# Orders of issue in the first stage of a hybrid retention and sparse-attention block: angle tables, variance, sine and gate stores

## The chip, the cores and the metric

The kernel runs on one core of a Trainium2 chip. The metric is device time in microseconds (us), the median of three runs. A core has five engines that run side by side and each issue their instructions in order: TensorE (PE, matmuls, and PEld, its weight loads), VectorE (DVE), ScalarE (ACT), GpSimd (POOL) and SyncE (SP), which here issues most transfers. They wait for each other through semaphores.

## The reference

One layer of a streaming encoder, 1024 positions of width 1024, all in float32. What matters here is its beginning:

```python
h = rms_norm(x, norm_mix)
proj = h @ w_in            # retention q, k, v, gate; sparse attention q, latent, k_pe, gate; indexer q, k, w
r_q, r_k = rotary(r_q, positions, 10000.0), rotary(r_k, positions, 10000.0)
q_pe, k_pe = rotary(d_q[..., :16], positions, 500000.0), rotary(d_pe, positions, 500000.0)
q_idx, k_idx = partial_rotary(i_q, ...), partial_rotary(i_k, ...)
ret = head_group_norm(retention(r_q, r_k, r_v), ret_norm) * silu(r_g)
score = sum over h of w_idx[h] * relu(q_idx[h] @ k_idx.T / sqrt(32))    # the indexer's scores
```

The 256 best keys of each query by `score` (chunk-causal) are attended to by the sparse heads; the outputs of both head groups go through an output projection, a gated embedding and a last norm. So the kernel needs the row's `rsqrt(mean(x*x))` (`rstd`), cosine and sine of two families of angles, the silu of the gate columns, and the indexer's rotated queries and keys before the first score.

## The kernel before

Matmuls of the projection run on split operands: each float32 is a high and a low part, and a product is three matmuls (high by high, high by low, low by high). The projection uses the unnormalised `x`; `rstd` is applied when a result is taken out of PSUM or through the angle tables.

The parts of the first stage, in the order of the program:

- Lines 288 to 300 load the transposed `x` in eight slices and the first weights `w_p1`, split them, and add up the squares in `acc`; `squares` is the last sum.
- Lines 305 to 314 accumulate the first projection block: two rotated halves in `P1` (PSUM tiles `big`) and the plain indexer columns in `PI[0]` (the two PSUM banks `nb`).
- `angles` and `tables` (lines 344 to 357) make a cosine and a sine table: VectorE multiplies the positions with the frequencies, reduces the angle to one turn in six instructions, ScalarE takes two sines and a square, VectorE makes the cosine of the square. `cosx`, `sinx` serve the sparse attention and the indexer, `cosr`, `sinr` retention.
- Lines 378 to 381 sum the squares over the partitions with matmuls (L380), and `rsqrt` makes `rstd`: a VectorE step (`rs_a`), a power on GpSimd (`rs_y`), four small VectorE steps. `spread` (line 364) spreads `rstd` over all partitions with matmuls (L368); ScalarE copies the result to `rstd_b`.
- `evacuate(0)` copies `PI[0]` to `it` on ScalarE (L375). It frees the two `nb` banks, which the gate chunk needs next.
- `t_block(12, ...)` is the second plain block of indexer columns; `put_plain` multiplies a block with `rstd_b`, splits it into `ih`, `il` and stores both to DRAM (`d_iq`, L407). `rotate` and lines 413 to 432 rotate `P1` (`xo`), split it (`xs`) and store the parts (`d_iq`, `d_ik`, `d_qs`, `d_kp`).
- `tables(cosr, sinr)` and their products with `rstd_b` (lines 433 to 435).
- Lines 446 to 474, the indexer's scores: `ks` and `qs` are loaded back from `d_ik` and `d_iq`, one matmul for each head (L466), a Relu on ScalarE (`rel`), a multiply-add on VectorE (`sc`).
- `n_chunk` (line 480): eight tiles of 128 rows and 256 columns, 24 matmuls each (L491 to L493), two tiles to a PSUM bank (`nb`, two buffers). ScalarE evacuates a tile with the chunk's function, for the gate chunks 2 and 3 the silu, into half of a buffer `nst` (three buffers, L495); GpSimd multiplies a full buffer with the norm's gain (L505), and SyncE stores it with two transfers (`d_g`, L510). Chunks run as 2, 3, 0, 1.

The program is not issued as written. A list scheduler puts the instructions of each engine in an order, by their place in the program and by when a model of their durations expects them to be ready; on the chip each engine then keeps that order, whatever is late. `with tc.issue_after(x)` and `add_manual_dep(..., NoSync, ...)` add an order of issue without a semaphore. `behind(ins, name)` notes an instruction, and `mark(name, last)` later orders all that were noted under that name behind `last`. The scores of the first two row tiles are so ordered behind the third tile of chunk 3 (`"chunk 3 tile 2"`).

Of the kernel before, what the change touches and what calls it, by code (L numbers as in the profile page):

```python
# [14 lines left out]
AF = mybir.ActivationFunctionType  # L15
# [138 lines left out]
def _body(ctx, nc, tc, ap, dbg):  # L154
    V, A, G, T, Y = nc.vector, nc.scalar, nc.gpsimd, nc.tensor, nc.sync

    def f(t):
        return t.bitcast(F32)
# [6 lines left out]

    def mark(name, ins):
        for x in marks.pop(name, []):
            tc.add_manual_dep(x.ins, ins.ins.name,
                              mybir.DependencyInfo(mybir.DependencyClass.NoSync, mybir.DependencyReason.DATA),
                              reason="order of issue")  # L170
# [157 lines left out]
    def rsqrt(out, ssum, n, w):  # L328
        a = tiny.tile([128, 16], F32, name="rs_a")[:, :w]
        y = tiny.tile([128, 16], F32, name="rs_y")[:, :w]  # L330
        z = tiny.tile([128, 16], F32, name="rs_z")[:, :w]
        V.tensor_scalar(a, ssum, 1.0 / n, EPS, op0=OP.mult, op1=OP.add)  # L332
        G.tensor_tensor(out=y, in0=a, in1=mhalf[:, :w], op=OP.pow)  # L333
        V.tensor_tensor(out=z, in0=y, in1=y, op=OP.mult)
        V.tensor_tensor(out=z, in0=z, in1=a, op=OP.mult)
        V.tensor_scalar(z, z, -0.5, 1.5, op0=OP.mult, op1=OP.add)
        V.tensor_tensor(out=out, in0=y, in1=z, op=OP.mult)
# [6 lines left out]
    def angles(col, cos_t):  # L344
        V.tensor_scalar(cos_t, posi, cst[:, CV + col:CV + col + 1], None, op0=OP.mult)

    def tables(cos_t, sin_t):
        ang, kk = cos_t, sin_t
        V.tensor_scalar(kk, ang, 1.0 / (2.0 * math.pi), MAGIC, op0=OP.mult, op1=OP.add)
        V.tensor_scalar(kk, kk, -MAGIC, None, op0=OP.add)  # L350
        for c in CODY:
            V.scalar_tensor_tensor(ang, kk, -c, ang, op0=OP.mult, op1=OP.add)
        V.tensor_scalar(ang, ang, PI_LO, -PI_LO, op0=OP.min, op1=OP.max)
        A.activation(sin_t, ang, AF.Sin)
        A.activation(cos_t, ang, AF.Sin, scale=0.5)
        A.activation(cos_t, cos_t, AF.Square)
        V.tensor_scalar(cos_t, cos_t, -2.0, 1.0, op0=OP.mult, op1=OP.add)

    with tc.issue_after(squares.ins):
        angles(1, cosx)  # L360
        tables(cosx, sinx)
        angles(0, cosr)

    def spread(dst, col):
        for h in range(2):
            pr = nb("ib")
            for j in range(4):
                T.matmul(pr[:, 128 * j:128 * j + 128], col[:, 4 * h + j:4 * h + j + 1].to_broadcast([128, 128]), ident,  # L368
                         start=True, stop=True)
            A.activation(dst[:, 512 * h:512 * h + 512], pr, AF.Copy)  # L370

    def evacuate(b):
        it = wk("it")
        for h in range(2):
            A.activation(it[:, 512 * h:512 * h + 512], PI[b][h], AF.Copy)  # L375
        return it
# [4 lines left out]
    rsqrt(rstd, pss[:, :NT], D, NT)  # L381
    spread(rstd_b, rstd)
    for t in (cosx, sinx):
        V.tensor_tensor(out=t, in0=t, in1=rstd_b, op=OP.mult)
    it0 = evacuate(0)
    PI.append([nb("ib"), nb("ib")])
    t_block(12, PI[1])
    it1 = evacuate(1)
# [13 lines left out]
    def put_plain(b, it):  # L402
# [3 lines left out]
        for n, t in enumerate((hi, lo)):  # L406
            Y.dma_start(d_iq[n, j0:j0 + nj].rearrange("j h t -> (j h) t"), f(t)[:8 * nj])  # L407
            if b == 1:
                Y.dma_start(d_ik[n, 8:32], f(t)[64:88])
# [23 lines left out]
    tables(cosr, sinr)  # L433
# [46 lines left out]
    def n_chunk(c, func, place=nb):  # L480
        ws = [load_w(ap["w_n"][c, kg], 256) for kg in range(4)]
        for tg in range(2):
            for a in range(4):
# [772 lines left out]
```

## Time and profile before

| | |
|---|---|
| median of three runs | 816.79 us (816.59 to 823.42) |
| the profiled execution | 815.47 us, of which 813.7 us from the first to the last instruction (the span) |
| TensorE busy | 755.0 us |
| VectorE busy | 587.5 us |
| ScalarE busy | 476.8 us |
| GpSimd busy | 312.5 us |
| mean granted TensorE clock | 0.977 of full |

All times inside the kernel are counted from the start of the span. The granted clock is the share of TensorE's full clock of 2.4 GHz that the chip allowed; 0.50 is its lower level, 1.2 GHz. A matmul's listed duration is longer than its distance from the next one, since matmuls are pipelined: distances between starts tell the pace. "Idle before" in a timeline is the time the engine stood still ahead of an instruction, with the instruction or transfer that ended it.

### The profile page before, as it was taken

The numbers are of one execution on the slowest core, as the hardware profiler recorded it, in microseconds if no ns is written. First come the engines' busy times: TensorE is split into PE (matmuls) and PEld (weight loads), VectorE is DVE, ScalarE is ACT, GpSimd is POOL, SyncE is SP. The second block draws the span as 40 slices with busy tenths as digits, with TensorE's granted clock in tenths as the row PEclk, the third lists the DMA queues.
The fourth block names the chain that finished last, engine by engine and source line by source line (L and its number), as shares of the span: only waits on it lengthen the run. The fifth ranks groups of instructions, "written<-read, shape, count | busy, mean of one in ns | idle before, by whom it ended". The sixth has DMA issues, their size and how long they took to land.

```text
span 813.7 us, 12654 instructions
## 1 busy us (share of the span) xinstructions
PE 755.0 (93%) x4415; PEld 653.5 (80%) x4415; DVE 587.5 (72%) x1270; ACT 476.8 (59%) x1041; POOL 312.5 (38%) x237
## 2 busy tenths in 40 slices
PE   9959499998999998999989888999999999899995
PEld 6858499987887887998788776878888887688885
DVE  5959058999999899999867877655565655644655
ACT  7544057638999599993666565543564544424333
POOL 2916245182765543740036668520261101310110
PEclk9969899998999999999999999999999999999999
DMA  8403733230532332531746565964445546542511
GB/s 317 123 21 109 189 101 96 78 98 27 145 114 79 117 104 89 173 119 52 194 111 189 171 190 162 268 233 149 160 168 191 168 163 218 195 156 78 180 52 52
DMA packets 65439, 113.89 MB, mean 140 GB/s; under 512 B 5888, under 2 KB 32896, under 8 KB 65376
## 3 DMA queue, kind: packets, MB, share of 16 engines
q1 hardware_dynamic: 61760, 106.53, 42.3%
q10 hardware_dynamic: 3616, 6.55, 2.2%
q8 instruction: 35, 0.57, 0.3%
q14 instruction: 28, 0.23, 0.1%
HBM read 75.45 MB, written 37.62 MB: 139 GB/s over the span
## 4 chain that ended last, share of the span: by engine, by line
PE 51%; DVE 31%; DMA 6%; ACT 4%; issue 4%; POOL 2%; SPq 1%; POOLq 0%; DVEq 0%; ACTq 0%
DVE res L645 8%; PE lg L1173 6%; PE rb L1173 5%; PE rb L1103 3%; PE rb L1104 3%; PE rb L1105 3%; DMA qk<-d_f 3%; PE tp L964 3%; DMA twr<-in_w_out 3%; PE nb L491 2%; PE nb L492 2%; PE nb L493 2%; DVE ad L654 2%; DVE sc L473 2%; DVE athr L656 2%
## 5 line engine op out<-in xcount | busy, mean ns | idle before, releaser
L235 POOL TENSOR_TENSOR wlo<-wraw,whi 128x512 fp32r<-128x512 f32 (+1 forms) x58 | 87.9, 1530 | 68.2 <-ACT whi L234 62.2
L661 ACT ACTIVATE ajunk<-key,cthr 128x1024 bf16<-128x1024 int16 (+5 forms) x96 | 95.5, 995 | 15.4 <-DVE key L622 10.5
L491 PE MATMUL nb<-whi,xhi 128*128 128x256 f32 x256 | 76.3, 300 | 22.8 <-ACT nst L495 14.1
L645 DVE TENSOR_SCALAR_CACHE_REDUCE res<-key,athr 128x384 f32<-128x384 int16 (+5 forms) x96 | 75.5, 786 | 2.1
L492 PE MATMUL nb<-wlo,xhi 128*128 128x256 f32 x256 | 75.6, 296 | 0.7 <-POOL wlo L235 0.7
L493 PE MATMUL nb<-whi,xlo 128*128 128x256 f32 x256 | 74.9, 295 | 0.0
L491 PEld LDWEIGHTS nb<-whi,xhi 128*128 128x128 f32 x256 | 52.1, 204 | 24.9 <-ACT nst L495 14.9
L333 POOL TENSOR_TENSOR rs_y<-rs_a,mhalf 128x1 f32<-128x1 f32 (+1 forms) x26 | 28.0, 1080 | 110.0 <-DVE rs_a L332 107.5
L971 DVE TENSOR_TENSOR t<-tp,t 128x512 fp32r<-128x512 f32 (+1 forms) x72 | 45.5, 643 | 29.7 <-ACT t L970 29.4
L947 ACT ACTIVATE lm<-lm,mxv 128x128 f32<-128x128 f32 (+3 forms) x64 | 49.4, 773 | 18.5 <-DVE mxv L946 17.0
L970 ACT ACTIVATE t<-tp 128x512 fp32r<-128x512 f32 (+1 forms) x72 | 38.9, 558 | 31.5 <-PE oo L1000 18.4
L322 PE MATMUL big<-xhi,whi 128*128 128x512 f32 x144 | 56.0, 391 | 0.5 <-DVE mb L399 0.5
L323 PE MATMUL big<-xlo,whi 128*128 128x512 f32 x144 | 56.2, 390 | 0.0
L324 PE MATMUL big<-xhi,wlo 128*128 128x512 f32 x144 | 55.7, 390 | 0.0
L473 DVE SCALAR_TENSOR_TENSOR sc<-rel,wi,sc 128x1024 f32<-128x1024 f32 (+5 forms) x42 | 51.0, 1214 | 4.3 <-ACT rel L469 1.6
L492 PEld LDWEIGHTS nb<-wlo,xhi 128*128 128x128 f32 x256 | 52.2, 204 | 1.9 <-POOL wlo L235 1.3
L493 PEld LDWEIGHTS nb<-whi,xlo 128*128 128x128 f32 x256 | 51.9, 203 | 0.6
L964 PE MATMUL tp<-cst,lm 128*128 128x128 f32 x288 | 46.8, 276 | 2.5 <-DVE t L971 2.0
L234 ACT ACTIVATE whi<-wraw 128x512 fp32r<-128x512 f32 (+1 forms) x58 | 34.9, 609 | 19.5 <-POOL cg L523 5.4
L943 DVE CUSTOM_DVE_ANT_0 lm<-lg,bias 128x512 f32<-128x512 f32 (+2 forms) x64 | 36.7, 585 | 11.9 <-PE tp L964 6.5
L1106 DVE TENSOR_TENSOR xt<-rb,xt 128x512 f32<-128x512 f32 x32 | 21.9, 689 | 30.3 <-PE rb L1105 25.9
L999 PE MATMUL oo<-t,vd 128*128 128x256 f32 (+1 forms) x144 | 38.1, 284 | 3.2 <-ACT t L970 2.9
(497 smaller groups left out, 2424.5 us busy)
## 6 DMA issues: line engine op xcount, KB each, us to landing
wraw<-in_w_t SPq DMA_DIRECT2D x26, 256.0 KB, 2.8
wraw<-in_w_n SPq DMA_DIRECT2D x24, 256.0 KB, 2.7
d_f<-o SPq DMA_DIRECT2D x8, 512.0 KB, 3.2
qk<-d_f SPq DMA_DIRECT2D x8, 512.0 KB, 4.9
ql<-d_qs SPq DMA_DIRECT2D x16, 256.0 KB, 4.5
qh<-d_qs SPq DMA_DIRECT2D x32, 128.0 KB, 4.9
twr<-in_w_out SPq DMA_DIRECT2D x8, 512.0 KB, 6.7
xt<-in_x SPq DMA_DIRECT2D x8, 512.0 KB, 4.3
```

What stands on the lines that cost most here:

```text
L235: G.tensor_tensor(out=lo, in0=raw, in1=f(hi), op=OP.subtract)
L322: T.matmul(outs[h], wh, xhi[k][:, sl], start=k == 0, stop=False)
L323: T.matmul(outs[h], wh, xlo[k][:, sl], start=False, stop=False)
L324: last = T.matmul(outs[h], wl, xhi[k][:, sl], start=False, stop=k == 7)
L473: V.scalar_tensor_tensor(dst, rel[:, :w], wi[:, i, h:h + 1], dst, op0=OP.mult, op1=OP.add)
L491: T.matmul(pb[:, a % 2], xhi[k][:, tsl], wh, start=k == 0, stop=False)
L492: T.matmul(pb[:, a % 2], xhi[k][:, tsl], wl, start=False, stop=False)
L493: last = T.matmul(pb[:, a % 2], xlo[k][:, tsl], wh, start=False, stop=k == 7)
L645: V.tensor_scalar(junk, src[:, KS[i]], thr[:, n:n + 1], 0.0, op0=op, op1=OP.add, accum_out=cnt[:, n:n + 1])
L661: A.activation(junk[:, :128 * (i + 1)], src[:, KS[i]], AF.Sign, bias=self.thr[:, n:n + 1], accum_out=cnt[:, n:n + 1])
L964: T.transpose(tp[:, o:o + 128], pt[a][:, ks_], ident)
L1173: T.matmul(po[c.start // 512][:, c.start % 512:c.start % 512 + c.stop - c.start], a, b[:, c], start=k == 0 and m == 0, stop=k == n - 1 and ...
```

## The change

Only orders of issue change; every instruction computes what it did.

1. In the first stage, after the sum of squares, VectorE is to do the first angle table (`cosx`) up to its last reduction (`reduced`), then the first step of `rsqrt` (`first`), then the angle of the second table (`turn`). The reductions of the second table come behind the last sum of the rotation (`turned`).
2. The first sine (`sine`) is issued behind the second copy of `it`.
3. The matmuls of the first `spread` are issued behind the last matmul of tile 0 of chunk 2.
4. The first store of the index path (the high part of `put_plain(0)`) is issued behind the second store of tiles 2 and 3 of chunk 2 (`"chunk 2 stored 3"`).

```diff
+    def queue(ins, first):
+        tc.add_manual_dep(ins.ins, first.ins.name, ...NoSync..., reason="order of issue")
...
-        V.tensor_scalar(a, ssum, 1.0 / n, EPS, op0=OP.mult, op1=OP.add)
+        first = V.tensor_scalar(a, ssum, 1.0 / n, EPS, op0=OP.mult, op1=OP.add)
...
+        return first, V.tensor_tensor(out=out, in0=y, in1=z, op=OP.mult)
...
-        V.tensor_scalar(ang, ang, PI_LO, -PI_LO, op0=OP.min, op1=OP.max)
-        A.activation(sin_t, ang, AF.Sin)
+        last = V.tensor_scalar(ang, ang, PI_LO, -PI_LO, op0=OP.min, op1=OP.max)
+        sin = A.activation(sin_t, ang, AF.Sin)
...
     with tc.issue_after(squares.ins):
         angles(1, cosx)
-        tables(cosx, sinx)
-        angles(0, cosr)
+        _, reduced, sine = tables(cosx, sinx)
+        turn = angles(0, cosr)
...
-    rsqrt(rstd, pss[:, :NT], D, NT)
-    spread(rstd_b, rstd)
+    first, scaled = rsqrt(rstd, pss[:, :NT], D, NT)
+    queue(first, reduced)
+    queue(turn, first)
+    spread(rstd_b, rstd, "chunk 2 tile 0")
...
-    it0 = evacuate(0)
+    it0, last = evacuate(0)
+    queue(sine, last)
...
-            Y.dma_start(d_iq[n, j0:j0 + nj].rearrange("j h t -> (j h) t"), f(t)[:8 * nj])
+            st = Y.dma_start(d_iq[n, j0:j0 + nj].rearrange("j h t -> (j h) t"), f(t)[:8 * nj])
+            if b == 0 and n == 0:
+                behind(st, "chunk 2 stored 3")
...
-        V.tensor_tensor(out=xo[:, :, sl], in0=two(ma), in1=two(mb), op=OP.add)
+        turned = V.tensor_tensor(out=xo[:, :, sl], in0=two(ma), in1=two(mb), op=OP.add)
...
-    tables(cosr, sinr)
+    first, *_ = tables(cosr, sinr)
+    queue(first, turned)
...
-                        Y.dma_start(dst[:, j - 1:j + 1], st.rearrange("p a (g c) -> g p a c", g=2)[a2])
+                        last = Y.dma_start(dst[:, j - 1:j + 1], st.rearrange("p a (g c) -> g p a c", g=2)[a2])
+                    mark(f"chunk {c} stored {j}", last)
```

## Rows read from the trace of the kernel before

**Rows 1.** The page: busy time and instructions by engine; granted clock in 40 slices.

```profile
PE 755.0 (93%) x4415; PEld 653.5 (80%) x4415; DVE 587.5 (72%) x1270; ACT 476.8 (59%) x1041; POOL 312.5 (38%) x237
...
PEclk9969899998999999999999999999999999999999
```

**Rows 2.** Timeline of TensorE: start us, us, instruction, idle before and its releaser.

```profile
50.29 0.58 PE L491 MATMUL nb<-whi,xhi 128*128 128x256 f32 x1 [8.73 <-ACT it L375]
...
56.32 0.28 PE L491 MATMUL nb<-whi,xhi 128*128 128x256 f32 x1
...
56.44 0.28 PE L492 MATMUL nb<-wlo,xhi 128*128 128x256 f32 x1
...
99.22 0.58 PE L491 MATMUL nb<-whi,xhi 128*128 128x256 f32 x1 [9.97 <-ACT nst L495]
...
108.59 1.09 PE L466 MATMUL big<-ks,qs 96*128 96x512 f32 x4
```

**Rows 3.** Stretches: us, busy us of PE, PEld, DVE, ACT, POOL (instructions); clock, DMA.

```profile
50.29:56.20 5.91, 5.91 (x27) 5.91 (x28) 1.57 (x6) 5.67 (x7) 2.06 (x2) 0.50 0.18 46
...
99.20:104.00 4.80, 4.78 (x22) 4.78 (x23) 0.00 (x0) 1.79 (x3) 2.39 (x2) 0.50 0.08 10
```

**Rows 4.** Timeline of ScalarE: the sine, a copy behind it, a table load.

```profile
48.70 1.06 ACT L354 ACTIVATE sinx<-cosx 128x1024 f32<-128x1024 f32 x1 [11.10 <-DVE cosx L353]
...
51.60 0.58 ACT L375 ACTIVATE it<-nb 128x512 f32<-128x512 f32 x1
...
60.12 1.28 ACT L495 ACT_TABLE_LOAD   x1
61.41 0.84 ACT L495 ACTIVATE nst<-nb,rstd 128x256 f32<-128x256 f32 x2
```

**Rows 5.** Timeline of VectorE: tables, variance, a product, the rotation's last sum.

```profile
34.26 1.78 DVE L345 TENSOR_SCALAR cosx<-posi,cst 128x1024 f32<-128x1024 int32 x1
...
39.36 0.68 DVE L349 TENSOR_SCALAR sinr<-cosr 128x1024 f32<-128x1024 f32 x1
...
42.30 1.21 DVE L352 SCALAR_TENSOR_TENSOR cosr<-sinr,cosr 128x1024 f32<-128x1024 f32 x1
...
49.18 0.15 DVE L332 TENSOR_SCALAR rs_a<-ib 128x8 f32<-128x8 f32 x1
...
51.71 0.17 DVE L337 TENSOR_TENSOR rstd<-rs_y,rs_z 128x8 f32<-128x8 f32 x1
...
63.54 1.22 DVE L435 TENSOR_TENSOR cosr<-cosr,rstd_b 128x1024 f32<-128x1024 f32 x1
...
74.81 3.42 DVE L416 TENSOR_TENSOR xo<-ma,mb 128x1024 f32<-128x1024 f32 x1
```

**Rows 6.** Timeline of SyncE's queue: index stores, weights, index loads, gate stores.

```profile
67.74 0.33 SPq L407 DMA_DIRECT2D d_iq<-ih  x1
...
71.48 2.69 SPq L231 DMA_DIRECT2D wraw<-in_w_n  x2
...
79.35 0.33 SPq L425 DMA_DIRECT2D d_iq<-xs  x1
...
91.75 0.56 SPq L453 DMA_DIRECT2D qs<-d_iq  x1
...
94.34 3.37 SPq L510 DMA_DIRECT2D d_g<-nst  x6
```

**Rows 7.** Chain of work, 30 to 125 us: start us, us, what.

```profile
94.99 3.60 DMA d_g<-nst
```

**Rows 8.** Waits, 30 to 125 us: total us, times, longest.

```profile
DVE sc L471 <- ACT rel L469: 27.4, 1, 27.4
```

**Rows 9.** Timeline of GpSimd: power of the variance, gate multiply of tiles 2, 3.

```profile
49.42 1.65 POOL L333 TENSOR_TENSOR rs_y<-rs_a,mhalf 128x8 f32<-128x8 f32 x1 [10.53 <-DVE rs_a L332]
...
81.71 2.27 POOL L505 TENSOR_TENSOR nst<-nst,retn_b 128x512 f32<-128x512 f32 x1
```

More of the change, by code (lines that the diff above doesn't have):

```diff
@@ L164, in behind @@
         marks.setdefault(mark, []).append(ins)
+    def queue(ins, first):
+        tc.add_manual_dep(ins.ins, first.ins.name,
+                          mybir.DependencyInfo(mybir.DependencyClass.NoSync, mybir.DependencyReason.DATA),
+                          reason="order of issue")
     def mark(name, ins):
         for x in marks.pop(name, []):
-            tc.add_manual_dep(x.ins, ins.ins.name,
-                              mybir.DependencyInfo(mybir.DependencyClass.NoSync, mybir.DependencyReason.DATA),
-                              reason="order of issue")
+            queue(x, ins)
     def pool(name, **kw):
@@ L336, in rsqrt @@
         V.tensor_scalar(z, z, -0.5, 1.5, op0=OP.mult, op1=OP.add)
-        V.tensor_tensor(out=out, in0=y, in1=z, op=OP.mult)
+        return first, V.tensor_tensor(out=out, in0=y, in1=z, op=OP.mult)
     cosr = rpool.tile([128, S], F32, name="cosr")
@@ L344, in angles @@
     def angles(col, cos_t):
-        V.tensor_scalar(cos_t, posi, cst[:, CV + col:CV + col + 1], None, op0=OP.mult)
+        return V.tensor_scalar(cos_t, posi, cst[:, CV + col:CV + col + 1], None, op0=OP.mult)
     def tables(cos_t, sin_t):
         ang, kk = cos_t, sin_t
-        V.tensor_scalar(kk, ang, 1.0 / (2.0 * math.pi), MAGIC, op0=OP.mult, op1=OP.add)
+        first = V.tensor_scalar(kk, ang, 1.0 / (2.0 * math.pi), MAGIC, op0=OP.mult, op1=OP.add)
         V.tensor_scalar(kk, kk, -MAGIC, None, op0=OP.add)
@@ L357, in tables, with spread @@
         V.tensor_scalar(cos_t, cos_t, -2.0, 1.0, op0=OP.mult, op1=OP.add)
+        return first, last, sin
     with tc.issue_after(squares.ins):
         angles(1, cosx)
-        tables(cosx, sinx)
-        angles(0, cosr)
-    def spread(dst, col):
+        _, reduced, sine = tables(cosx, sinx)
+        turn = angles(0, cosr)
+    def spread(dst, col, at=None):
         for h in range(2):
@@ L367, in spread @@
             for j in range(4):
-                T.matmul(pr[:, 128 * j:128 * j + 128], col[:, 4 * h + j:4 * h + j + 1].to_broadcast([128, 128]), ident,
-                         start=True, stop=True)
+                m = T.matmul(pr[:, 128 * j:128 * j + 128], col[:, 4 * h + j:4 * h + j + 1].to_broadcast([128, 128]),
+                             ident, start=True, stop=True)
+                if at:
+                    behind(m, at)
             A.activation(dst[:, 512 * h:512 * h + 512], pr, AF.Copy)
@@ L374, in evacuate @@
         for h in range(2):
-            A.activation(it[:, 512 * h:512 * h + 512], PI[b][h], AF.Copy)
-        return it
+            last = A.activation(it[:, 512 * h:512 * h + 512], PI[b][h], AF.Copy)
+        return it, last
     pss = nb("ib")
@@ L380, in _body @@
         T.matmul(pss[:, j:j + 1], acc[:, 128 * j:128 * j + 128], ones1, start=True, stop=True)
-    rsqrt(rstd, pss[:, :NT], D, NT)
-    spread(rstd_b, rstd)
+    first, scaled = rsqrt(rstd, pss[:, :NT], D, NT)
+    queue(first, reduced)
+    queue(turn, first)
+    spread(rstd_b, rstd, "chunk 2 tile 0")
     for t in (cosx, sinx):
         V.tensor_tensor(out=t, in0=t, in1=rstd_b, op=OP.mult)
-    it0 = evacuate(0)
+    it0, last = evacuate(0)
+    queue(sine, last)
     PI.append([nb("ib"), nb("ib")])
     t_block(12, PI[1])
-    it1 = evacuate(1)
+    it1, _ = evacuate(1)
     def two(t):
```

## The prediction, on record before the result was known

> **What bounds the kernel now.** I read the page first: TensorE is busy for 93% of the span and VectorE for 72%, so a gain has to come from TensorE's idle time or from work of VectorE that ends last. The page's clock line shows two places below full speed in the first eighth of the span [rows 1], so I went to the timeline of TensorE there. It has two holes. The first matmul of the gate stage (line 491) starts at 50.29 us after 8.73 us of idleness, and the view names ScalarE's copy `it` as what released it. A second hole of 9.97 us ends at 99.22 us, released by ScalarE's `nst` [rows 2]. Behind each hole the granted clock stands at 0.50 of full, that is 1.2 GHz: 27 matmuls take 5.91 us and 22 take 4.78 us [rows 3], where the same matmul later follows the one before it by 0.12 us (56.32 to 56.44) [rows 2]. At 0.12 us they would take 3.24 and 2.64 us, so the slow stretches cost 2.67 and 2.14 us.
>
> Why the first hole: ScalarE issues in order, and the sine of line 354 sits ahead of both copies of `it`. It waits 11.10 us for VectorE, runs at 48.70, and the copies follow, the second from 51.60 [rows 4]. VectorE is late because two angle tables go through it in turns: the first starts at 34.26 and the variance (`rs_a`) comes behind both at 49.18, so `rstd` is written only at 51.71 [rows 5].
>
> Why the second: `nst` has three buffers, and the evacuation of tile 6 needs the one whose two stores (`d_g`) stand in SyncE's queue behind all stores and loads of the index path. They are issued from 94.34 [rows 6], land 3.60 us after 94.99 [rows 7], and tile 7 of the same bank follows at 99.22 [rows 2]. VectorE meanwhile waits 27.4 us for the first scores [rows 8], which TensorE reaches at 108.59 [rows 2]. Both engines therefore wait for this stage, and what it loses shifts the rest of the kernel.
>
> **The change, part by part.**
>
> *One table first, variance between, sine behind the copies.* The copies of `it` need only the last projection matmuls. TensorE runs out of work at 50.29 - 8.73 = 41.56 us [rows 2]; the copies can be done by then, so the gate tiles start there instead of at 50.29, and at the full clock, since nothing has stood still. Gain: 8.73 + 2.67 = 11.4 us. `rstd` comes earlier too. From 34.26: one angle at 1.78, the two scalings at 0.68 to 1.78 each (0.68 is the row of the second table, 1.78 the first row, beside GpSimd's work), three of 1.21 and the clamp at 0.68 [rows 5], together 7.5 to 9.7; with the middle, 8.6, the table is reduced at 43 us. Then `rs_a` at 0.15, GpSimd's power at 1.65 [rows 9], and the steps up to `rstd`: in the trace `rs_a` to the end of `rstd` is 49.18 to 51.88, 2.7 us [rows 5]. `rstd` is there at about 46. The angle of the other table fits into the 1.65 of the power.
>
> *Spread behind tile 0.* 24 matmuls at 0.12 put the end of tile 0 at 41.56 + 2.9 = 44.5, and the spread that stands behind it waits for `rstd` until 46: a new wait of 1.5 us. If the compiled order puts tile 2 between, it is nothing; if `rstd` takes the long bound, 2.3. I take 1.5. Net of this part 9.9 us.
>
> *The second table behind the rotation.* Its six reductions move from before 49 us to behind the last sum `xo` (74.81) [rows 5]; one after another they are 5.7 us, and two products with `rstd_b` at 1.22 leave the stretch ahead of the rotation, which brings the index path forward by up to 2.4 us more. Cover: VectorE's 27.4 us of waiting for scores [rows 8]; the consumer, `cg` of retention (line 523), stands behind the score and value stages in the program. Without that cover the whole table costs 5.7 + 0.7 + 2.4 = 8.8 us of VectorE in a stage that it bounds. On ScalarE the split of the sines brings two more table loads, 1.28 us each [rows 4]. I take 0 for both, as the remaining hole (below) hides them, and up to 8.6 in a rival.
>
> *Gate stores ahead.* One store, the high half of the first index block (67.74 in the trace), is tied behind the second store of tile 3. The gate multiply that this store needs is at 81.71 for 2.27 us [rows 9], so done at 74.1 us once it is 9.9 us earlier. Three orders are possible in SyncE's queue. (a) The other index stores, being ready, go first; then gate stores of tiles 0 to 3, the tied store, and the loads `qs`. The gate stores then overtake only the four `qs` loads, 94.34 - 91.75 = 2.6 us [rows 6], and the hole shrinks from 9.97 to 7.4. (b) All of the index path waits for 74.1. The gate hole is then gone, but the queue's issues of 79.35 to 94.34, without a wait of some 2 us in them, are 13 us, and the earlier ones (two stores at 0.33, two weight loads in 2.69, a store pair of the like) some 4: `qs` would be issued at 91 and land some 4 us later (3.60 is the nearest row) [rows 6, 7], while TensorE, 22.0 us earlier than at 108.59, stands before its scores at 86.6: a hole of 8.4. (c) The gate stores slip in between the index stores at 70 to 75, nothing else waits, and next to nothing of the hole is left. I take (a), 7.4: a queue that has work of its own ready for 13 of 15 us leaves little room for (c).
>
> *Sum.* The holes and slow stretches are 8.73 + 2.67 + 9.97 + 2.14 = 23.5 us. Less 1.5 for the spread and 7.4 for the hole that stays: 14.6. The shorter hole need not bring the slow clock back; if it does, 2.1 of it are lost. All is read from one execution of 815.47 us (span 813.7, so 1.8 around it), 1.3 below the median of 816.79; the difference goes on the median: 816.8 - 14.6 = 802.2.
>
> **Rivals.**
>
> *Both holes close.* The gate stores leave at 70 to 75 and the index loads land before 87. For it: index data are ready earlier by 9.9 to 12.3 us, and the transfers themselves need 3.6. Against it: those 15 us of issues have one gap, of 2 us. 816.8 - 23.5 + 1.5 = 794.8.
>
> *Only the first hole closes.* The store order comes out as before, or the hole moves to the scores at full size with its slow clock. 816.8 - 9.9 = 806.9.
>
> *ScalarE waits for VectorE again.* The second pair of sines may be put ahead of an evacuation. It then waits for up to 5.7 us of the table, and its two loads (2.6) and three passes of 1.06 follow: 11.5 us, of which one tile (2.9) is covered by the other bank: 8.6 us, 810.8. Without the wait it is 2.9, and hidden in the hole. For it: the first hole is just this. Against it: nothing else of that stage is late, and an order made by a model can put the sines where the table is done. The Trainium skill speaks against the change here: "ScalarE: Activation LUTs", section "Table sets: the hidden batching unit", says to batch by table set, and this splits one batch of sines into two. The same page, section "What ACT_TABLE_LOAD costs", adds 1.38 us of drain to each load; by that it would be 813.6. Here the first evacuation starts 1.29 us after its load starts (60.12 to 61.41) [rows 4], so the row shows the load alone.
>
> *Slower: the whole index path is held by the gate store.* If (b) holds and the gate multiply itself comes late on GpSimd, every microsecond passes on to the scores. In (b) the scores come about 21 us after the store; they are no earlier than the present 108.59 when it leaves at 88 us, and the kernel is 1% slower (825) from 96 us on. For it: one queue, in order. Against it: the multiply is at 81.71 even now, and its inputs come earlier.
>
> **How the numbers follow.** Chances: forecast 0.47 (798 to 806), both holes closed 0.22, only the first 0.11, ScalarE again 0.12, slower 0.08. The likeliest is 802.2. The range runs from nothing new lost, 816.8 - 23.5 = 793, to the ScalarE case with a little more, 812; what is left out is the slower case and some of the ends, under 2 in 10. A change of 1% (8.2 us) is about what a measurement of this kernel can tell from none: faster means below 808.6. That holds for the forecast, for both holes closed and for part of "only the first": 0.74. Same 0.18, slower 0.08.
>
> **What would show it.** TensorE's first gate matmul at 41.6 instead of 50.29 with no slow stretch behind it; `rs_a` near 43 and `rstd` near 46; a sine that starts behind both copies of `it`; the second table on VectorE between the last `xo` and the first score; `d_g` stores in SyncE's queue ahead of `qs`; a hole of some 7 us, before tile 7 or before the first scores, which come near 94. I am wrong if the first gate matmul still waits, if the scores do not come at least 10 us earlier, or if the later stages, which the change does not touch, give the shift back.

## The result, and the profile after

| | before | after |
|---|---|---|
| median of four runs on one chip | 819.44 us (816.59 to 823.42) | 808.08 us (806.26 to 811.39) |
| the profiled execution | 815.47 us, span 813.7 | 808.18 us, span 806.4 |
| mean granted clock | 0.977 | 0.980 |

The ratio of the times is 0.9871, with a 95% interval from 0.9835 to 0.9906: the change takes off 1.3%, 11.4 us between the medians. The forecast was 802.2 with a range of 793 to 812. Some executions below ran in a slower state of the chip and are left out of every median and ratio; of the first and the fourth experiment only times are told, since the profiled execution was one of these.

The page of the changed kernel, its busy times and its clock line (to be held against [rows 1]):

```profile
PE 755.7 (94%) x4415; PEld 656.1 (81%) x4415; DVE 591.8 (73%) x1270; ACT 477.0 (59%) x1041; POOL 313.2 (39%) x237
...
PEclk9999799999999999999999999999999999999998
```

No engine does less; TensorE stands still less. The low slice of the clock line that came from the first hole is gone, and the one in the fifth slice has stayed. The timeline of TensorE, changed kernel (start us, us, instruction, idle before and its releaser), answers [rows 2]:

```profile
41.28 0.36 PE L504 MATMUL nb<-whi,xhi 128*128 128x256 f32 x1
...
48.92 2.02 PE L373 MATMUL ib<-cst,rstd 128*128 128x128 f32 x16 [1.64 <-issue]
...
52.97 0.40 PE L326 MATMUL ib<-xhi,whi 128*128 128x512 f32 x1
...
84.30 0.58 PE L504 MATMUL nb<-whi,xhi 128*128 128x256 f32 x1 [5.08 <-ACT nst L508]
...
96.73 1.17 PE L479 MATMUL big<-ks,qs 96*128 96x512 f32 x4 [3.29 <-DMA qs<-d_iq]
```

Stretches of the same kernel (us, busy us of PE, PEld, DVE, ACT, POOL with instructions; granted clock; DMA share; GB/s), against [rows 3]:

```profile
41.28:47.28 6.00, 5.99 (x50) 5.79 (x49) 4.36 (x7) 3.18 (x4) 2.47 (x2) 1.00 0.18 44
84.30:88.20 3.90, 3.90 (x18) 3.90 (x19) 1.45 (x2) 2.98 (x4) 1.33 (x2) 0.51 0.88 224
...
98.40:101.80 3.40, 3.40 (x18) 3.40 (x17) 2.98 (x3) 1.99 (x4) 0.00 (x0) 0.50 0.36 127
```

The first gate matmul starts 9.0 us earlier, at 41.28, with no wait over 0.6 us ahead of it, and at full clock. Two waits are left in series where the second hole was: 5.08 us on a gate evacuation and 3.29 us on the query load. Behind each the clock is at half, behind the first at once, behind the second from 98.40, 1.7 us after the wait ended. At 0.12 us a matmul, 18 would take 2.16 us; they take 3.90 and 3.40, so the slow stretches cost 1.74 and 1.24.

These rows close the sum of the first stage. Before, the two holes and their slow stretches were 23.5 us. After, the waits ahead of the first score are 1.64 + 5.08 + 3.29 = 10.01 and the slow stretch between them 1.74, together 11.75. The difference is 11.8, and the first score comes 108.59 - 96.73 = 11.9 us earlier. With the 1.24 behind the scores, 10.5 us remain: VectorE's twenty-first multiply-add of the scores follows at 134.49 instead of 144.80, 10.3 earlier. The end of this execution is only 7.3 us earlier than that of the execution before, so in this pair the later stages give back 3.0 us; among other things the granted clock is 0.97 from 430 to 490 us and 0.93 from 490 to 515, where it was 1.00 in these stages before, and TensorE waits 3.5 us on `vd` at line 761, where the longest such wait was 1.6 before. But the execution before lay 4 us below its median, with a mean clock of 0.977, as high as any execution of that kernel shows. Between the medians (11.4 us, by the interval 7.7 to 13.5) a loss behind the first stage does not show; one trace of each does not settle whether a typical execution has one.

ScalarE, changed kernel, against [rows 4]:

```profile
40.13 0.58 ACT L382 ACTIVATE it<-nb 128x512 f32<-128x512 f32 x1
...
44.77 1.06 ACT L358 ACTIVATE sinx<-cosx 128x1024 f32<-128x1024 f32 x1 [2.75 <-DVE cosx L357]
...
48.89 1.28 ACT L508 ACT_TABLE_LOAD   x1 [0.88 <-DVE rstd L341]
...
76.99 0.47 ACT L508 ACTIVATE nst<-nb,rstd 128x256 f32<-128x256 f32 x1 [5.45 <-PE nb L506]
82.82 1.06 ACT L358 ACTIVATE sinr<-cosr 128x1024 f32<-128x1024 f32 x1 [5.36 <-DVE cosr L357]
83.79 0.46 ACT L508 ACTIVATE nst<-nb,rstd 128x256 f32<-128x256 f32 x1
```

The first sine stands behind both copies, as meant. The second sine stands ahead of an evacuation (83.79) and waits 5.36 us for VectorE: this is the wait of 5.08 on TensorE. Between the evacuation at 76.99 and this sine there is no table load.

VectorE, changed kernel, against [rows 5], then GpSimd, against [rows 9]:

```profile
44.65 0.16 DVE L336 TENSOR_SCALAR rs_a<-ib 128x8 f32<-128x8 f32 x1
...
48.05 0.69 DVE L361 TENSOR_SCALAR cosx<-cosx 128x1024 f32<-128x1024 f32 x1 [0.47 <-ACT cosx L360]
48.65 0.16 DVE L341 TENSOR_TENSOR rstd<-rs_y,rs_z 128x8 f32<-128x8 f32 x1
...
67.27 2.32 DVE L428 TENSOR_TENSOR xo<-ma,mb 128x1024 f32<-128x1024 f32 x1
69.51 2.89 DVE L353 TENSOR_SCALAR sinr<-cosr 128x1024 f32<-128x1024 f32 x1
...
72.44 1.67 DVE L354 TENSOR_SCALAR sinr<-sinr 128x1024 f32<-128x1024 f32 x1
74.03 3.42 DVE L430 TENSOR_TENSOR xs<-xo,xs 128x1024 fp32r<-128x1024 f32 x1
```

```profile
44.89 2.09 POOL L337 TENSOR_TENSOR rs_y<-rs_a,mhalf 128x8 f32<-128x8 f32 x1 [3.22 <-DVE rs_a L336]
...
71.81 1.74 POOL L518 TENSOR_TENSOR nst<-nst,retn_b 128x512 f32<-128x512 f32 x1
```

`rstd` is 3.1 us earlier than before, and its last step stands behind the cosine of the first table (48.05), which waits for ScalarE's square. Two reductions of the second table (69.51 and 72.44) stand between the last sum `xo` and its split `xs`, which is what the index path waits for. SyncE's queue and the chain of work, changed kernel, against [rows 6, 7]:

```profile
68.53 1.58 SPq L523 DMA_DIRECT2D d_g<-nst  x2
...
86.27 0.94 SPq L523 DMA_DIRECT2D d_g<-nst  x2
87.25 0.50 SPq L417 DMA_DIRECT2D d_iq<-ih  x1
...
90.76 0.56 SPq L466 DMA_DIRECT2D qs<-d_iq  x1
```

```profile
69.59 2.82 DVE sinr L353
...
87.25 3.50 DMA d_iq<-ih
91.36 5.23 DMA qs<-d_iq
```

The gate stores of tiles 0 and 1 leave at 68.53, ahead of nearly the whole index path; those of tiles 2 and 3 leave at 86.27, then the tied store, and the query load can go only when that store has landed (87.25 + 3.50 = 90.75). The chain that ended last runs through just these: the reductions, the tied store, the query load. And the cover of [rows 8] has shrunk from 27.4 us to 7.8 (the wait of VectorE's first score step in the list of waits; the store named there is what came last by the profile, not what the step needs):

```profile
DVE sc L484 <- DMA d_g<-nst: 7.8, 1, 7.8
```

### The profile page after: what moved, and what is told of

Same layout as the page of the kernel before. It is cut to its first block, busy times and chain, and to the rows that moved or that the text cites. A ratio compares the mean times of both kernels' runs of the same rounds, so it can differ in the third digit from the quotient of the medians.

```text
span 806.4 us, 12657 instructions
## 1 busy us (share of the span) xinstructions
PE 755.7 (94%) x4415; PEld 656.1 (81%) x4415; DVE 591.8 (73%) x1270; ACT 477.0 (59%) x1041; POOL 313.2 (39%) x237
## 4 chain that ended last, share of the span: by engine, by line
PE 62%; DVE 18%; DMA 8%; ACT 4%; issue 3%; POOL 2%; SPq 1%; ACTq 0%; POOLq 0%; DVEq 0%
PE lg L1187 6%; PE rb L1187 5%; PE rb L1117 4%; PE rb L1118 4%; PE rb L1119 4%; PE tp L978 3%; PE big L328 3%; PE big L327 3%; PE big L326 3%; DVE res L659 3%; PE nb L504 2%; PE nb L505 2%; PE nb L506 2%; DMA qk<-d_f 2%; DMA twr<-in_w_out 2%
## 5 line engine op out<-in xcount | busy, mean ns | idle before, releaser
L675 ACT ACTIVATE ajunk<-key,cthr 128x1024 bf16<-128x1024 int16 (+5 forms) x96 | 95.5, 995 | 14.9 <-DVE key L636 10.5
L504 PEld LDWEIGHTS nb<-whi,xhi 128*128 128x128 f32 x256 | 50.9, 199 | 10.8 <-ACT nst L508 9.7
L486 DVE SCALAR_TENSOR_TENSOR sc<-rel,wi,sc 128x1024 f32<-128x1024 f32 (+5 forms) x42 | 51.0, 1214 | 5.8 <-ACT rel L482 3.0
L957 DVE CUSTOM_DVE_ANT_0 lm<-lg,bias 128x512 f32<-128x512 f32 (+2 forms) x64 | 36.7, 584 | 13.5 <-PE tp L978 7.5
L978 PEld LDWEIGHTS tp<-cst,lm 128*128 128x128 f32 x288 | 34.7, 144 | 8.7 <-DVE t L985 5.3
```

The costliest lines, as they stand in the source:

```text
L486: V.scalar_tensor_tensor(dst, rel[:, :w], wi[:, i, h:h + 1], dst, op0=OP.mult, op1=OP.add)
L504: T.matmul(pb[:, a % 2], xhi[k][:, tsl], wh, start=k == 0, stop=False)
L675: A.activation(junk[:, :128 * (i + 1)], src[:, KS[i]], AF.Sign, bias=self.thr[:, n:n + 1], accum_out=cnt[:, n:n + 1])
L978: T.transpose(tp[:, o:o + 128], pt[a][:, ks_], ident)
```

## The experiments

The theory after the result: the first hole was closed by the orders on VectorE and ScalarE; of the second hole, one part is now the second sine waiting for its reductions, the other the query load waiting for the tied store. The rival: what is left of the second hole is still the gate stores' place in SyncE's queue. The experiments undo or add one part at a time. "First score" is the first matmul of line 479 in the changed kernel.

One fact of the compiled programs matters throughout. An edit in the first stage can change the order that the list scheduler gives to the stages long behind it. For each kernel I compared the order of TensorE's instructions with that of the changed kernel, by tenths of the program (1.00: all stand in the same order):

```
kernel before                 .80 .99 1.0 1.0 1.0 1.0 1.0 1.0 1.0 1.0
without the tie               same as changed in all tenths
sine behind tile 6            same as changed in all tenths
sine behind tile 7 (1 and 3)  1.0 .45 .59 .99 .99 1.0 .54 .60 .85 .85
first sine free (7)           .92 1.0 1.0 1.0 1.0 1.0 .54 .60 .85 .85
sine alone (8), and run 4     .99 1.0 1.0 1.0 1.0 1.0 .65 .54 .85 .85
tie alone (9)                 .80 1.0 1.0 1.0 1.0 1.0 .60 .51 .85 .85
```

Runs 1, 3 and 7 have the very same order in the last four tenths; runs 4 and 8 share another, run 9 has a third. The order in which the matmuls start in the traces groups the kernels in the same way. Kernels without a line here (6, 10, 11, 12) keep the changed kernel's order behind the first two tenths.

**Run 1: the second sine later.** To take the wait of 5.36 off the evacuations:

```diff
-    first, *_ = tables(cosr, sinr)
+    first, _, sine = tables(cosr, sinr)
+    behind(sine, "chunk 2 taken 7")    # marked at the evacuation of tile 7
```

> The changed kernel with one edit: the second pair of sines is ordered behind the evacuation of tile 7 of chunk 2, so that ScalarE no longer waits 5.36 us for VectorE ahead of the evacuation of tile 6. Theory (two waits in series on the way to one event, the first scores, and the later one, the loads qs that land near 96.6 us, decides): the hole of 5.08 us before 84.30 goes, TensorE reaches the scores near 87 and waits there until 96 to 97, the first score stays at 96.7 within 1 us and the time within 2 us of the changed kernel (806 to 810). Rival (ScalarE's wait is what keeps the gain from its forecast size): the first score comes at 90 and the time falls by 5 to 7 us, to 801 to 803.

818.79 us, ratio to before 1.0025 (0.9995 to 1.0055): the whole gain is gone. Neither theory foresaw that. It led to the comparison of the compiled orders, and to runs 5 and 7.

**Run 2: without the tie of the first index store.**

```diff
-            if b == 0 and n == 0:
-                behind(st, "chunk 2 stored 3")
```

> The changed kernel without the tie of the first index store to the gate stores of tiles 2 and 3 (the other orders stay). Theory (the gate stores of the first two tiles come early because their evacuation does, not because of the tie; the tie only puts 3.5 us of a late store ahead of the loads qs): qs are issued near 86.5 instead of 90.8, the first scores come 2 to 4 us earlier (93 to 95), the gate stores of tiles 2 and 3 land near 92 and hold the evacuation of chunk 3's first tile by 2 to 4 us; the time is 804 to 808. Rival (the tie is what shrinks the second hole): a hole of 7 us or more returns before tile 7 and the time is 811 or more.

803.63 us, ratio 0.9828 (0.9789 to 0.9867). SyncE's queue and TensorE of this kernel:

```profile
85.74 0.56 SPq L464 DMA_DIRECT2D qs<-d_iq  x1
```

```profile
83.76 0.58 PE L502 MATMUL nb<-whi,xhi 128*128 128x256 f32 x1 [5.08 <-ACT nst L506]
```

The query load leaves 5.0 us earlier than with the tie, and the wait of 3.29 ahead of the scores is gone; the first score is at 93.57. The gate stores of tiles 0 and 1 still leave at 68.01. So the tie costs 3.2 us at the first score, and the early gate stores don't come from it. The differences of the medians are 2.2 apart, the same way, but less than their uncertainty. The later stores now hold an evacuation of ScalarE for 3.11 us, as expected, but TensorE does not wait for it. The wait of 5.08 is unchanged, which excludes the rival: the gate stores are early, and the evacuation waits all the same.

**Run 3: run 1, and the second table's reductions behind the split.** `queue(first, turned)` becomes `queue(first, parted)`, where `parted` is the last instruction that writes the low half of `xs`.

> As the late sine, and the reductions of the second table are ordered behind the split of the rotated block (xs) on VectorE instead of behind its sum xo. Theory (two of these reductions, 2.82 and 1.61 us, stand between xo and its split and hold the whole index path): the split starts near 70.7 instead of 74.03, every store behind it and the loads qs come 3 to 4 us earlier, the first score near 93, and the time is 803 to 806. Rival (SyncE's queue and the transfers set when qs land, not the split): the first score stays at 96 to 97 and the time at 806 to 810.

The first stage did as the theory said: the split at 70.38 instead of 74.03, the first score at 93.00, 15.6 us earlier than before. The time did not: 817.85 us, ratio 0.9997 (0.9973 to 1.0021). The loss lies hundreds of microseconds later. TensorE's two longest waits there, in this kernel:

```profile
477.43 0.61 PE L850 MATMUL rb<-cst,qk 128*128 128x128 f32 x3 [4.08 <-DMA qk<-d_f]
...
537.01 0.79 PE L1119 MATMUL rb<-wo0h,mTh 128*128 128x512 f32 x1 [5.29 <-ACT mTh L1109]
```

Neither the kernel before nor the changed one has a wait over 2.5 us on TensorE between 400 and 610 us.

**Run 4: run 3 with the tie moved to the stores of tiles 0 and 1** (`"chunk 2 stored 1"`).

> As the last, and the first index store is tied behind the stores of tiles 0 and 1 only. Theory (the late tied store, 3.5 us to land, stands ahead of qs): qs are issued near 83 and land near 88, TensorE reaches the scores at 87, the first score comes at 88 to 90 and the time is 798 to 802. Rival (the gate stores of tiles 2 and 3, now behind qs, hold the evacuations of chunk 3): a hole of 5 us or more opens around the first scores, and the time is 803 to 808.

802.98 us, ratio 0.9822 (0.9783 to 0.986), between the two ranges expected. It differs from run 3 in one order, the gate stores behind which the first index store stands, and is 14.9 us faster. In the first stage run 3 has only one wait over 1.6 us left (2.35 us, ended at 88.63, with a granted clock of 0.68 in the 5.4 us behind it), so the first stage can account for some 4 us at most. That the rest is the other order of the later stages was inferred here; runs 5 and 7 test it.

**Run 5: the second sine behind tile 6.** Run 1 with `"chunk 2 taken 6"`; the later order is that of the changed kernel.

> The changed kernel with the second sine ordered behind the evacuation of tile 6 of chunk 2 instead of tile 7 (that was the earlier run with the late sine); here every engine's compiled order behind the first stage is the one of the changed kernel. Theory (the late sine lost its gain because the scheduler re-ordered the later stages): the wait of 5.08 us before the tile at 84.30 shrinks to 0 to 3, the query load still leaves near 90 because it stands behind the tied store, so the first score comes at 94 to 97 and the time is 804 to 808. Rival (a late second sine costs time by itself, for instance because its table is late for whoever reads it): 815 to 820, as the run with tile 7.

807.88 us, ratio 0.986 (0.9797 to 0.9924), against 818.79 for run 1, which places the same sine one tile later. A late sine does not cost the gain by itself: here it kept it, and in run 3, with the sine behind tile 7, the first score came 15.6 us earlier. What runs 1 and 3 have and this run has not is the other later order. TensorE of this kernel:

```profile
85.35 0.58 PE L505 MATMUL nb<-whi,xhi 128*128 128x256 f32 x1 [3.46 <-ACT whi L238]
...
95.85 1.16 PE L480 MATMUL big<-ks,qs 96*128 96x512 f32 x4 [2.92 <-DMA qs<-d_iq]
```

As for the first stage, the wait of 5.08 became one of 3.46 on converted weights, which stand behind the sine on ScalarE, and the scores still wait for the query load (2.92): the first score is at 95.85, only 0.9 us earlier than in the changed kernel, since the load, behind the tied store, sets it.

**Run 6: no tie, and the reductions behind the split.**

> The changed kernel without the tie of the first index store, and with the second table's reductions behind the split of xo instead of behind xo; every engine's compiled order behind the first stage is the one of the changed kernel. Theory (reductions of 4.6 us in front of the split delay the index path by some 3.5): the split at 70.4 instead of 73.5, the query load at 82 to 83 instead of 85.7 of the run without the tie; the first score at 89 to 92 (93.57 there), 799 to 802. Rival (the transposing engine's own wait for the second sine sets the scores, and that waits for the same reductions, now later): first score at 93 to 95, 803 to 806.

800.16 us, ratio 0.9784 (0.9732 to 0.9836): the lowest time of the study, 18.5 us below the medians of before. VectorE and TensorE of this kernel:

```profile
70.42 2.22 DVE L428 TENSOR_TENSOR xs<-xo,xs 128x1024 fp32r<-128x1024 f32 x1 [1.03 <-ACT xs L427]
```

```profile
84.30 0.51 PE L503 MATMUL nb<-whi,xhi 128*128 128x256 f32 x1 [2.51 <-ACT whi L238]
...
86.17 0.58 PE L504 MATMUL nb<-wlo,xhi 128*128 128x256 f32 x1 [1.36 <-POOL wlo L239]
```

The split is 3.1 us earlier than in run 2 and the query load leaves at 83.30, 2.4 us earlier. The first score, at 92.69, gains only 0.9, since TensorE is now late by itself: behind the second sine, which still waits for VectorE, stand the weight conversions of the next chunk. That is the rival's mechanism and the theory's time; the first score lies between the two ranges. The median is 3.5 us below that of run 2, more than the first score shows; each has an uncertainty of some 4 us.

**Run 7: the changed kernel without the order of the first sine** (`queue(sine, last)` left out).

> The changed kernel without the edit that queues the first sine behind the copies. The compiled order still has both copies ahead of the sine, so the first stage keeps its gain (first gate matmul at 40 to 42, first score at 94 to 99); but behind tenth 6 of the program the compiled order of every engine is the one of the two slow runs with the late sine, not that of the changed kernel. Theory (that order costs 11 to 14 us between 430 and 600): 815 to 821. Rival (the order of the later stages costs nothing, and those runs lost for another reason): 806 to 811.

Ratio 1.0028 (0.9995 to 1.0061), median 821.89. Two things are read from it, and one of them goes against the text of the expectation, which was wrong on the compiled order: without the edit the sine stands ahead of the copies. TensorE of this kernel:

```profile
46.83 0.58 PE L503 MATMUL nb<-whi,xhi 128*128 128x256 f32 x1 [5.58 <-ACT it L382]
...
483.44 0.90 PE L847 MATMUL rb<-cst,qk 128*128 128x128 f32 x3 [5.30 <-DMA qk<-d_f]
...
542.53 0.50 PE L1116 MATMUL rb<-wo0h,mTh 128*128 128x512 f32 x1 [3.77 <-ACT mTh L1106]
```

First, one angle table first, without the order of the sine, shortens the first hole from 8.73 to 5.58 and no more. Second, the scores come 7.3 us earlier than before and the kernel ends later than before: the two long waits of run 3 are here too, on the same lines of the program, with the same later order and another first stage. Held against the shift of the first scores (the table below), this later order costs 10 us here and 16 in run 3; which difference in it makes the load of `qk` late was not followed.

**Run 8: the order of the first sine alone**, on the kernel before.

```diff
-        A.activation(sin_t, ang, AF.Sin)
+        sin = A.activation(sin_t, ang, AF.Sin)
...
-    it0 = evacuate(0)
+    it0, last = evacuate(0)
+    queue(sine, last)    # written out with add_manual_dep
```

> The kernel before with one edit alone: the sine queued behind the copies. The second table stays early, the variance and the stores are as before; the compiled order of the last four tenths is that of the run with the tie at tile 1. Theory (the first hole of 8.73 with its slow clock is worth 9.9 and needs only this edit): first gate matmul at 41, first score 9 to 11 earlier than before, 805 to 809. Rival (the sine behind the copies only helps when the second table is out of the way): first score 3 to 6 earlier, 811 to 815.

807.37 us, ratio 0.9865 (0.981 to 0.992): one of the four edits gives as much as all four. But not for the reason expected. TensorE, ScalarE and SyncE's queue of this kernel:

```profile
50.28 1.06 PE L495 MATMUL nb<-whi,xhi 128*128 128x256 f32 x2 [7.12 <-ACT whi L234]
...
95.30 1.80 PE L470 MATMUL big<-ks,qs 96*128 96x512 f32 x4 [1.81 <-DMA qs<-d_iq]
```

```profile
48.65 1.06 ACT L354 ACTIVATE sinr<-cosr 128x1024 f32<-128x1024 f32 x1 [8.17 <-DVE cosr L353]
49.62 0.61 ACT L234 ACTIVATE whi<-wraw 128x512 fp32r<-128x512 f32 x1
...
56.76 0.84 ACT L499 ACTIVATE nst<-nb,rstd 128x256 f32<-128x256 f32 x2
57.49 1.12 ACT L371 ACTIVATE rstd_b<-ib 128x512 f32<-128x512 f32 x2
```

```profile
75.56 1.25 SPq L514 DMA_DIRECT2D d_g<-nst  x2
```

The first hole is not closed, it is moved: the gate matmuls start at 40.77 and stop at 43.16 for 7.12 us, because the next weights' conversion stands behind the other table's sine, which waits for VectorE as before. What is gone is the second hole, 9.97 us and its slow clock. The first two evacuations now stand ahead of the copies to `rstd_b` (56.76 and 57.49; before, the first stood behind them, at 61.41 [rows 4]), and the stores of tiles 0 and 1 leave at 75.56 instead of 94.34. The buffers `nst` are free in time, so tile 6 does not wait for one. The first score matmul comes 13.3 us earlier than before, more than the 9 to 11 expected, but the stretch from 95.30 to 99.00 runs at a clock of 0.54, and the first multiply-add of the scores is 10.7 us earlier.

**Run 9: the tie alone**, on the kernel before.

> The kernel before with one edit alone: the first index store tied behind the gate stores of tiles 0 to 3. The compiled order of the stores is the one that the prediction took as (a): the other index stores first, then the gate stores of tiles 0 to 3, the tied store, the query load. Theory (the prediction's term for the second hole): first hole unchanged (first gate matmul at 50), gate stores at 90 to 92 instead of 94.3, second hole 7 to 8 instead of 9.97, first score 2 to 3 earlier, 814 to 818 (its later order differs in tenths 7 and 8 from that of before). Rival (the query load, now behind the tied store's round trip, sets the scores): query load at 95 or later, first score at 101 to 112 with a wait on that load in front of it, 816 to 822.

820.05 us, ratio 1.0005 (0.9971 to 1.004). TensorE and SyncE's queue of this kernel:

```profile
95.70 0.58 PE L493 MATMUL nb<-whi,xhi 128*128 128x256 f32 x1 [6.13 <-ACT nst L497]
```

```profile
92.09 2.03 SPq L512 DMA_DIRECT2D d_g<-nst  x4
94.17 0.49 SPq L407 DMA_DIRECT2D d_iq<-ih  x1
...
97.40 0.56 SPq L455 DMA_DIRECT2D qs<-d_iq  x1
```

In the first stage the tie does by itself what the prediction said of it, in the order (a): the gate stores overtake the query loads, the hole shrinks to 6.13, the first score comes 3.6 us earlier, each a little beyond the range expected. The time is not in the theory's range: the later order gives the gain back, with a wait of 4.35 on the load of `qk` at 485.85 and one of 3.21 at 541.27.

**Run 10: no tie, and the second table's reductions behind the last step of `rstd`** (`queue(first, scaled)`).

> The changed kernel without the tie, and with the second table's reductions behind the last step of the inverse root instead of behind xo, where VectorE has idle stretches of 3.2 (before 51.7) and 3.7 (before 62.4); the compiled order behind the first stage is that of the changed kernel. Theory (both waits of the run with the split first, 2.51 and 1.36 near 85, come from the second sine being late): second sine at 53 to 57, no wait over 0.6 on TensorE between 60 and the scores but for the query load, first score at 87 to 91 (92.69 there), 795 to 798. Rival (the reductions delay the index path on VectorE): split of xo at 73 or later instead of 70.42, first score at 92 to 95, 800 to 804.

804.48 us, ratio 0.9804 (0.9765 to 0.9844): near the rival's time. VectorE and TensorE of this kernel:

```profile
75.55 2.21 DVE L428 TENSOR_TENSOR xs<-xo,xs 128x1024 fp32r<-128x1024 f32 x1 [1.02 <-ACT xs L427]
```

```profile
91.89 2.04 PE L477 MATMUL big<-ks,qs 96*128 96x512 f32 x4 [4.84 <-DMA qs<-d_iq]
```

Both waits near 85 are gone, as the theory said; but the table's work on VectorE pushes the split from 70.42 to 75.55, the query load leaves at 87.04, and TensorE waits 4.84 us for it (first score at 91.89). The idle stretches of VectorE were too short for the table.

**Run 11: run 10, and the first table's cosine behind `rstd`** (`queue(done, scaled)`, `done` being line 361's instruction).

> As the run before in this list, and the first table's last step (the cosine, which waits for ScalarE's square) queued behind the last step of the inverse root, which in the changed kernel stands behind it. Theory (that wait made rstd late: 48.36 instead of 47.3): rstd at 47.0 to 47.6, the wait of 1.66 before the spread at 0.3 to 1.0, first score 0 to 1.5 earlier than in the run before, 794 to 798. Rival (the wait before the spread is filled either way, or the evacuation of the second tile, which now comes behind the copies of the spread, delays the gate stores and opens the second hole again): same time or 2 to 6 slower, with a wait on a gate evacuation between 75 and 95.

803.68 us, ratio 0.9797 (0.9762 to 0.9832). From the start of `rs_a` to that of the last step of `rstd` it is 2.96 us (45.20 to 48.16) instead of 4.00 (45.45 to 49.45), and the wait ahead of the spread shrinks from 1.66 to 0.98: the cosine's step did hold it. But the first score is at 92.38, no earlier than in run 10, and the time is that of run 10 within the uncertainty, as the rival said. Two other waits of 1.60 and 1.04 appear near 74.

**Run 12: run 6, and the second sine behind the last weight conversion of chunk 3.**

> The changed kernel without the tie, with the second table's reductions behind the split of xo (the run of 800.16), and with the second sine queued behind ScalarE's conversion of the last weight block of chunk 3; the compiled order behind the first stage is that of the changed kernel. Theory (the waits of 2.51 and 1.36 near 85 are weight conversions that stand behind the waiting second sine, with the slow clock after them): both waits gone, no stretch at half clock before the scores or only a short one, query load still at 83, so the first score is set by its landing at 88 to 90.5 instead of 92.69, and the time is 795 to 798.5. Rival (the converted weights or the query load are late for another cause): first score at 92 to 93, 799 to 802.

802.9 us, ratio 0.9831 (0.979 to 0.9873). TensorE of this kernel:

```profile
87.61 0.58 PE L504 MATMUL nb<-whi,xhi 128*128 128x256 f32 x1 [3.75 <-ACT nst L508]
```

The waits of 2.51 and 1.36 are gone, and one of 3.75 stands in their place: the evacuation of tile 7, also behind the sine. The first score is where it was (92.62). The theory failed; the rival's first score fits (its time does not quite, 802.9 for 799 to 802), by a cause that it did not name. The second sine is late on VectorE, and in each of its places on ScalarE (the changed kernel, runs 3, 5, 6 and 12) something that TensorE needs stands behind it.

**All together.** The shift of VectorE's first multiply-add of the scores (L486; 99.45 in the changed kernel, 111.24 before), and the difference of the medians:

| kernel | shift of the first multiply-add | difference of medians |
|---|---|---|
| later order as in the changed kernel | | |
| changed kernel | -11.8 | -11.4 |
| 5: sine behind tile 6 | -12.7 | -10.8 |
| 2: no tie | -14.6 | -13.6 |
| 6: no tie, split first | -15.9 | -18.5 |
| 12: and sine behind weights | -16.0 | -15.6 |
| 10: no tie, table at `rstd` | -14.9 | -15.4 |
| 11: and cosine last | -13.9 | -16.2 |
| another later order | | |
| 8: sine alone | -10.7 | -11.3 |
| 9: tie alone | -3.6 | +0.2 |
| 7: first sine free | -7.2 | +3.2 |
| 3: late sine, split first | -15.5 | +0.6 |

In the upper part the time follows the first scores within 2.6 us. In the lower part it does so for one order of three. A difference of medians is itself uncertain by some 4 us.

## Why the prediction was right, and where not

**What bounds the kernel.** Right: both holes were worth their length to the whole kernel. The table shows that what the first stage gains the time gains, within 2.6 us, as long as the later order is kept.

**One table first and the sine behind the copies: 11.4 us.** Right in sum: first gate matmul at 41.28 (41.6 foretold), full clock. Not right if it were read as two gains: the order of the sine alone leaves a hole of 7.12 a little later (run 8), one table first without it leaves 5.58 (run 7). Only both together close it, because after the copies the weight conversions stand in the same queue.

**`rstd` at 46.** Wrong: 48.65. `rs_a` came at 44.65 for 43, the power took 2.09 for 1.65, and the last step stood behind the cosine's (run 11), which the prediction had not looked for: it is a wait that VectorE takes on ScalarE in the middle of `rsqrt`.

**Spread: 1.5 us.** Measured 1.64, but at 48.92 and not at 44.5: the compiled order put tile 2 ahead of the spread, which would have made the wait nothing, and `rstd` was late by more than its long bound. Two errors that cancel. The net of 9.9 stands: the second projection block starts 7.5 us earlier (52.97 for 60.50), with 18 more gate matmuls (2.2 us) already done by then, together 9.7.

**Second hole: 7.4 left.** The size was close, the cause was another. The order (a) came, but for tiles 0 and 1, whose stores had already gone at 68.53. The gate multiply of tiles 2 and 3 started at 71.81, 9.9 us earlier than before, just as foretold. With the buffers free, the rest of the hole is the rival "ScalarE waits for VectorE again": 5.36 us of waiting for `cosr`, foretold as up to 5.7. That rival's price of 8.6 was too high, since the two table loads (2.6 us) did not come and only one of the three passes stood ahead of the evacuation. The second part, 3.29, is the query load's wait for the tied store. The prediction's order (b) had the landing of that load in it (some 4 us), its order (a) nothing of the kind, and neither the wait of the load for the store. So 8.37 lies near 7.4 by luck: two waits that the forecast had not put there came in place of the one that it had.

**The slow clock: 0.** This is the term that was most mis-sized. The prediction wrote that a shorter hole need not bring the slow clock back. It came back behind both waits, 1.74 and 1.24 us. The sum with the measured terms: 23.5 - 1.64 - 8.37 - 2.98 = 10.5 instead of 14.6, and 816.8 - 10.5 = 806.3, against 808.08 measured. The rest is within the uncertainty: one more execution moved the median before from 816.79 to 819.44.

**The second table at 0.** Half right. The cover of 27.4 us is there for most of it, but the queue of VectorE is in order: two reductions of 4.6 us (2.89 + 1.67) stood ahead of the split, on the path to the scores. Together with the tie they cost what run 6 gets back: 4.1 us at the first multiply-add, and a time of 800.16, near the 802.2 that the prediction had given to the change.

**Two more table loads at 0, with up to 2.6 in a rival.** They do not exist: the sine at 82.82 runs under the table loaded for the silu at 48.89. The Trainium skill, "ScalarE: Activation LUTs", section "Table sets: the hidden batching unit", says that functions of one set need one load. The trace agrees with that rule (one load of 1.28 us, then silu and sine in turns); the prediction had read the load between the sines and the silu in [rows 4] as a change of sets in both directions, and here the table loaded for the silu served the sine too.

**Later stages.** The prediction named their giving back as what would make it wrong. Between the medians of the changed kernel that does not show, and the change happened to leave their order alone; in the profiled pair 3.0 us of 10.3 are given back. Runs 1, 3 and 7 show that this was not safe: an edit of one order in the first stage re-ordered them, and the whole gain went.

**The tie.** As a part of this change it was a loss of 3.2 us at the first score (run 2): the stores of tiles 0 and 1 were early without it, TensorE waited for no later one, and it put the query load behind a late store. Alone it is a gain of 3.6 in its stage (run 9). The prediction priced it on the kernel before, where it helps, and did not ask what the other parts would leave for it to do.

## What to carry to other kernels

When a list scheduler sets the order, look at the compiled order of the whole program behind an edit, not only near it: with the first stage 15 us shorter, a re-ordered later stage made the same kernel no faster than before. When an instruction that waits for another engine is moved in an in-order queue, ask what stands behind it in the new place; three places for the same sine gave three waits of 2.5 to 5.1 us, on one tile's evacuation, on converted weights, on the next tile's evacuation. Price each edit once more on the kernel that the other edits leave, and try each alone: one of four here gave the whole gain, and one took some of it away (the first and the third were not tried alone).

## What the runs showed of the hardware

- TensorE's granted clock stood at 0.50 to 0.51 behind waits of 5.08 and of 3.29 us, for 18 matmuls each time; behind the wait of 1.64 it stayed at full. The number is not fixed by the wait: behind another wait of 5.08, in run 2, it was 27 matmuls (0.50 from 83.76 to 89.50), as many as behind the hole of 8.73 before.
- A silu and a sine shared one loaded table: no load between the evacuation at 76.99 and the sine at 82.82.
- A store to DRAM and a load of the same tensor behind it took 3.50 and 5.23 us in the chain of work, with the DMA engines busy to 0.84 from 88.20 to 93.44 and to 0.87 from 90 to 97. The Trainium skill, "DMA: Bandwidth & Descriptors", section "Latency and other measured facts", says that the latency of the memory grows from 0.2 us to 2 under high load. No run here parts that latency from the rest of a transfer; the rows are longer than its figure.
- A scaling step of VectorE of one shape took 0.68 us in [rows 5], 1.67 in the changed kernel (72.44) and 2.77 in run 6 (74.38), the latter two beside GpSimd's work (rows of 2.85 us from 73.51 and from 73.75). The table's six reductions, 5.7 us by the rows before, took 9.97 in run 6 (1.78 + 2.77 + 4.73 + 0.69).
